# Layer 1 of a two-layer mixer trunk: the rotary exchange by GpSimd's transfers in place of ScalarE's copies

## The chip, the cores and the metric

The kernel runs on one core of one Trainium2 chip. Its time is the device time of one execution in microseconds (us), and the times below are the median of several runs and one profiled execution.

## What is computed

Two layers of a mixer over 256 latent positions and 256 context positions of width 2048, in fp32. Each layer normalizes the stream, projects it by one wide matrix, and sends the columns of the projection through three branches: a gated MLP that mixes positions, windowed attention with grouped heads (8 query heads, 2 key heads of 128), and a Fourier mix. Each branch is multiplied by its own gate, and one output projection returns to width 2048. Queries and keys of the latent positions are turned by a rotary embedding before the scores are taken:

```python
def rope_2d(x, cos, sin):
    shp = x.shape
    xf = x.astype(jnp.float32).reshape(*shp[:-1], 2, 2, ROPE_FREQS)
    rot = jnp.stack([-xf[..., 1, :], xf[..., 0, :]], axis=-2).reshape(shp)
    out = xf.reshape(shp) * cos[None, :, None, :] + rot * sin[None, :, None, :]
    return out.astype(x.dtype)
```

A head has 128 numbers in four groups of 32. For `rot`, groups 0 and 1 change places, and groups 2 and 3; the sign is in the sine table. The result leaves only the latent stream, so the context stream of the second layer (layer 1 here) gives keys and values and nothing else.

## The kernel before, in words

**How the numbers are held.** Activations lie with the width on the 128 partitions and positions along the free axis, so one query head of layer 1 is a tile of 128 partitions by 256 positions. Products are fp32 by parts: a number is split into a rounded high half (ScalarE, L615 or L566 for weights) and the low half, the remainder (VectorE, L616 or L568). A product is then three matmuls: high by high, high by low, low by high (L598, L599, L600). Wide units of layer 1 use L754 and L755.

**Layer 1's units.** `tunit1` computes 128 columns of the projection as 16 pairs of matmuls. Its weights come in two pieces of 512 KB, loaded by SyncE and split by ScalarE and VectorE three pieces ahead. The result is brought together by `joined`: ScalarE copies one part out of PSUM (L760) into a tile `join` in SBUF, of which there are two, and VectorE adds the other part (L761). Units run in the order: two key units, the values, eight query units, eight gate units.

**The turning.** `rope` (L1118 and on) has the `join` tile as `ps`. Four copies by ScalarE (L1125) put each group of 32 partitions into its partner's place in `rot`, one of four tiles that are parts of one called `mgl`. VectorE multiplies `join` by the cosines (L1127), `rot` by the sines (L1128) and adds the two (L1129). ScalarE rounds the sum to the high half, VectorE takes the low half; both are read by the scores.

**The scores.** `attention` is a generator. TensorE's order is written out by hand: after a query's unit, a clock of nominal PE time (`YQ`, 6.8 us in layer 1) decides behind which matmuls of the next units its scores are put, and the other steps of the softmax follow in the same manner. The scores of one head are two groups of three matmuls (`ps_sc`, L598 to L600): the first two read the query's high half, the third its low half. VectorE then adds the mask (L1147), takes maxima (L1149) and their least (L1159, `nm`), ScalarE takes exponentials (L1162, L1169), VectorE the reciprocal of their sums (L1172, L1173), ScalarE multiplies (L1178), and TensorE transposes the result (L1198).

**Who sets which order.** TensorE's order is the program's. In this stage the orders of VectorE, ScalarE, GpSimd and SyncE are made by a scheduler when the program is built; on the chip every engine keeps its order, and an instruction that waits holds up all that is queued behind it on its engine. Beside the heads, VectorE sums up the gate of the output in small steps (L362, L364), which are put between its other work.

**GpSimd's queue.** Before layer 1's key units GpSimd has asked for 28 transfers that add the input to a tile as they land (L1472, L1483); behind them it has one small power (L628) and then nothing until the end.

Of the kernel before, what the change touches and what calls it, by code (L numbers as in the profile page):

```python
# [16 lines left out]
S = 256  # L17
# [49 lines left out]
def trunk_kernel(ctx: ExitStack, tc: tile.TileContext, xT, xhalf, cT, wss, wsl, wmod, win, wout0, wout1, const, vec, rows,  # L67
                 wmat, bs, sink, out):
    nc = tc.nc
    V, A, G, PE, DMA = nc.vector, nc.scalar, nc.gpsimd, nc.tensor, nc.sync  # L70
# [6 lines left out]
    def sb(shape, dt, tag, bufs=1):  # L77
        cnt[0] += 1
        return pool.tile(shape, dt, tag=tag, bufs=bufs, name=f"{tag}_{cnt[0]}")

    def w2k(shape, dt=F32):
        return sb(shape, dt, "w2k", W2K)
# [71 lines left out]
    def cc(name):  # L154
        o, w = COFF[name]
        return cst[:, o - P:o - P + w]
# [457 lines left out]
    def split_into(hi, lo, src):  # L614
        A.copy(hi, src)  # L615
        V.tensor_tensor(out=lo, in0=src, in1=hi.bitcast(F32), op=ALU.subtract)  # L616
        return hi, lo
# [122 lines left out]
    def tunit(n, sl=None):  # L740

        sl = slice(0, n) if sl is None else sl
        ps = mm_ps("t")
        for k in range(KT):
            if k % 8 == 0:
                w = W.next()
            c = slice((k % 8) * P, (k % 8 + 1) * P)
            mm3(ps[:, sl], part(w, c), (hh[k][:, sl], hl[k][:, sl]), k == 0, k == KT - 1)
            later.tick(PASS * n)
        return ps  # L750
# [13 lines left out]
    def tunit1(streams):  # L764

        pss = [mm_ps("t") for _ in streams]
        for k in range(KT):
            if k % 8 == 0:
                w = W.next()
            for s, ps in zip(streams, pss):  # L770
                mm2(ps, part(w, slice((k % 8) * P, (k % 8 + 1) * P)), (hh, hl)[s][k], k)
                later.tick(PASS * S)
        return [joined(ps) for ps in pss]
# [12 lines left out]
    def layer(l):  # L786
        last = l == 1
# [4 lines left out]
        if last:  # L792
            a = sb([P, 4, 256], F32, "macc")
# [323 lines left out]
        def rope(hi, lo, ps, ctx=None):  # L1117

            if ctx is None and hi.shape[-1] > S:
                ctx = ps[:, S:T]  # L1120
            nrot[0] += 1
            rot = rots[nrot[0] % 4]
            for a in range(4):
                b = a ^ 1
                A.copy(rot[32 * a:32 * a + 32], ps[32 * b:32 * b + 32, 0:S])  # L1125
            t = w2k([P, S])
            V.tensor_tensor(out=t, in0=ps[:, 0:S], in1=cc("cos"), op=ALU.mult)  # L1127
            V.tensor_tensor(out=rot, in0=rot, in1=cc("sin"), op=ALU.mult)  # L1128
            V.tensor_tensor(out=rot, in0=rot, in1=t, op=ALU.add)  # L1129
            split_into(hi[:, LAT], lo[:, LAT], rot)  # L1130
            if hi.shape[-1] > S:
                split_into(hi[:, CTX], lo[:, CTX], ctx)
# [4 lines left out]
        def attention(h, ps):  # L1137
            g = h // 4
            q = w2k([P, n], F32R), w2k([P, n], F32R)
            rope(*q, ps)  # L1140
            yield YQ[l]
            sc, mx = [], sb([P, 4], F32, "mx", 2)
# [78 lines left out]
        for h in range(len(au), 4):  # L1221
            ps = tunit1([0])[0] if last else tunit(n)
# [3 lines left out]
        for g in range(4):  # L1226
            ps = tunit1([0])[0] if last else tunit(n)
# [3 lines left out]
        for h in range(4):  # L1231
            ps = tunit1([0])[0] if last else tunit(n)
            gate(h, ps)
        state["phase"] = f"cg{l}"
        for g in range(4):
            ps = tunit1([0])[0] if last else tunit(n)
# [6 lines left out]
        for j in range(2):  # L1243
            pss = tunit1([0, 1]) if last else [tunit(T)]
            kt.append((sb([P, T], F32R, f"kt{j}"), sb([P, T], F32R, ("ws", "bsb")[j])))
            rope(*kt[j], *pss)
# [16 lines left out]
        for h in range(8):  # L1263
            ps = tunit1([0])[0] if last else tunit(n)
# [3 lines left out]
        for h in range(8):  # L1268
            ps = tunit1([0])[0] if last else tunit(n)
# [251 lines left out]
    with tc.manual_schedule(engines={EN.PE}):  # L1521
# [47 lines left out]
        ps = sums  # L1569
# [106 lines left out]
```

## Time and profile before

| | |
|---|---|
| median of 3 runs | 1114.19 us (1113.49 to 1114.28) |
| the profiled execution | 1113.58 us, of which its span is 1111.8 us |
| TensorE's granted clock | 1.000 |
| layer 1's first and last exchange copy | 861.0 us, 962.1 us |
| scores of the first and the last query head start | 905.62 us, 966.15 us |

Times inside the profile count from the start of the span. A row of the timeline has the start, the length, the engine, the line, the operation and the tiles (written, then read), and in brackets how long the engine stood idle before it, and who released it. Since an engine starts an instruction while the last one ends, the time that an instruction really holds the engine is read from start to start. PE is TensorE, DVE VectorE, ACT ScalarE, POOL GpSimd and SP SyncE.

### The profile page before, as it was taken

How to read it: one execution, taken by the hardware profiler on the slowest of the kernel's cores; microseconds unless marked ns; L12 is line 12 of the kernel's file. 1: busy time of each engine (PE TensorE's matmuls, PEld its weight loads, DVE VectorE, ACT ScalarE, POOL GpSimd, SP SyncE). 2: the span in 40 equal slices, each digit the busy share in tenths (PEclk: the TensorE clock that was granted, in tenths of full speed). 3: DMA queues.
4: the chain of work that ended last, by engine and by line, in shares of the span. 5: the costliest groups of instructions: out<-in, count | busy, mean ns of one | idle time of the engine just before them, and what ended most of it. 6: DMA issues, size and time to landing. Idle time of an engine off the chain costs nothing. (4 is left out here: it accounts for less than half of the span.)

```text
span 1111.8 us, 17330 instructions
## 1 busy us (share of the span) xinstructions
PE 1102.6 (99%) x6437; PEld 925.4 (83%) x6437; DVE 927.2 (83%) x1609; ACT 553.3 (50%) x1060; POOL 33.3 (3%) x43
## 2 busy tenths in 40 slices
PE   8999999999999999999999999999999999999998
PEld 4787888888888888888888888988988888898886
DVE  3677799999988897989999998396989789878883
ACT  4455823322335667632533334266665379867551
POOL 1000000000000000000000000030500000000000
PEclk9999999999999999999999999999999999999999
DMA  9999765666665343466567675276956676576971
GB/s 376 414 414 409 248 194 184 190 209 212 187 208 159 124 143 115 143 195 194 160 206 220 201 225 171 95 184 202 234 168 207 217 222 198 166 241 210 313 253 75
DMA packets 75526, 235.89 MB, mean 212 GB/s; under 512 B 8481, under 2 KB 15025, under 8 KB 75441
## 3 DMA queue, kind: packets, MB, share of 16 engines
q1 hardware_dynamic: 71088, 230.31, 62.5%
q0 software_dynamic: 4064, 3.69, 2.2%
q8 instruction: 50, 0.82, 0.3%
q10 hardware_dynamic: 288, 0.79, 0.2%
q14 instruction: 36, 0.29, 0.1%
HBM read 232.65 MB, written 2.10 MB: 211 GB/s over the span
## 5 line engine op out<-in xcount | busy, mean ns | idle before, releaser
L566 ACT CAST whi<-raw 128x1024 fp32r<-128x1024 f32 (+1 forms) x210 | 216.7, 1035 | 308.9 <-PE ps_t L599 208.9
L598 PE MATMUL ps_t<-hh,whi 128*128 128x512 f32 (+1 forms) x752 | 290.6, 386 | 0.0
L600 PE MATMUL ps_t<-hh,wlo 128*128 128x512 f32 (+1 forms) x752 | 289.5, 385 | 0.0
L599 PE MATMUL ps_t<-hl,whi 128*128 128x512 f32 (+1 forms) x752 | 289.2, 385 | 0.0
L568 DVE TENSOR_TENSOR wlo<-raw,whi 128x1024 fp32r<-128x1024 f32 (+1 forms) x210 | 250.7, 1197 | 46.0 <-ACT whi L566 41.0
L323 DVE SCALAR_TENSOR_TENSOR macc<-mraw,cs,macc 128x512 f32<-128x512 f32 x360 | 251.2, 743 | 9.1 <-DMA mraw<-in_wmod_dram 8.8
L754 PE MATMUL ps_t<-hh,whi 128*128 128x512 f32 x512 | 180.7, 393 | 0.0
L600 PEld LDWEIGHTS ps_t<-hh,wlo 128*128 128x128 f32 x752 | 141.2, 188 | 28.8
L598 PEld LDWEIGHTS ps_t<-hh,whi 128*128 128x128 f32 x752 | 141.2, 188 | 26.6
L599 PEld LDWEIGHTS ps_t<-hl,whi 128*128 128x128 f32 x752 | 141.2, 188 | 26.3
L755 PE MATMUL ps_t<-hh,wlo 128*128 128x256 f32 x512 | 141.9, 277 | 0.0
L754 PEld LDWEIGHTS ps_t<-hh,whi 128*128 128x128 f32 x512 | 96.2, 188 | 19.2
L755 PEld LDWEIGHTS ps_t<-hh,wlo 128*128 128x128 f32 x512 | 96.2, 188 | 0.4
L598 PE MATMUL ps_y<-whi,hh 128*128 128x512 f32 x104 | 41.3, 397 | 0.0
L600 PE MATMUL ps_y<-whi,hh 128*128 128x512 f32 x104 | 40.6, 390 | 0.0
L599 PE MATMUL ps_y<-wlo,hh 128*128 128x512 f32 x104 | 40.5, 390 | 0.0
L615 ACT CAST w2k<-ps_tp 128x512 fp32r<-128x512 f32 x40 | 23.4, 584 | 21.0 <-PE ps_scc L599 13.6
L616 DVE TENSOR_TENSOR w2k<-ps_tp,w2k 128x512 fp32r<-128x512 f32 x40 | 27.4, 684 | 2.7 <-ACT w2k L615 1.7
L628 POOL TENSOR_TENSOR rs_b<-rs_a,mhalf 128x2 f32<-128x2 f32 (+1 forms) x7 | 6.3, 900 | 750.2 <-DVE mx L1446 582.9
L1178 ACT ACTIVATE w2k<-w2k,den 128x512 f32<-128x512 f32 (+1 forms) x48 | 28.1, 645 | 0.7 <-DVE den L1173 0.6
L833 PE MATMUL ps_av<-whi,hh 128*128 128x512 f32 x64 | 24.4, 396 | 0.2 <-ACT hh L703 0.2
L598 PE MATMUL ps_o<-w2k,vv 128*128 128x256 f32 x80 | 24.3, 304 | 0.0
(498 smaller groups left out, 1798.1 us busy)
## 6 DMA issues: line engine op xcount, KB each, us to landing
raw<-in_win_dram SPq DMA_DIRECT2D x158, 512.0 KB, 4.3
mraw<-in_wmod_dram SPq DMA_DIRECT2D x128, 512.0 KB, 4.4
raw<-in_wout_dram SPq DMA_DIRECT2D x60, 512.0 KB, 4.5
mraw<-in_wsl_dram SPq DMA_DIRECT2D x12, 512.0 KB, 7.2
yy<-in_xhalf_dram SPq DMA_DIRECT2D x7, 512.0 KB, 7.4
mg<-in_wsl_dram SPq DMA_DIRECT2D x7, 512.0 KB, 8.7
mgl<-in_wsl_dram SPq DMA_DIRECT2D x7, 512.0 KB, 9.2
yy<-in_xhalf_dram POOLq DMA_DIRECT2D x28, 128.0 KB, 7.6
```

The source lines that it names most:

```text
L323: V.scalar_tensor_tensor(out=acc[:, s], in0=w[:, kk % 2], scalar=c, in1=acc[:, s], op0=ALU.mult, op1=ALU.add)
L566: self.rounded = A.copy(ph, rc)
L568: self.last = V.tensor_tensor(out=pl, in0=rc, in1=ph.bitcast(F32), op=ALU.subtract)
L598: PE.matmul(ps, st[0], mv[0], start=start, stop=False)
L599: PE.matmul(ps, st[0], mv[1], start=False, stop=False)
L600: PE.matmul(ps, st[1], mv[0], start=False, stop=stop)
L615: A.copy(hi, src)
L616: V.tensor_tensor(out=lo, in0=src, in1=hi.bitcast(F32), op=ALU.subtract)
L754: PE.matmul(ps, w[0], h, start=k == 0, stop=False)
L755: PE.matmul(ps[:, 0:S], w[1], h[:, 0:S], start=False, stop=k == KT - 1)
L833: PE.matmul(ps, st[a], mv[b], start=start and (a, b) == (0, 0), stop=stop and (a, b) == (1, 0))
L1178: A.activation(prob[i][:, b * w:(b + 1) * w], prob[i][:, b * w:(b + 1) * w], AF.Copy, scale=den[:, c:c + 1])
```

## The change

In layer 1 the four copies of each exchange become four transfers from SBUF to SBUF, each of 32 partitions by 1 KB, asked for by GpSimd. Layer 0 keeps the copies: there the source lies in PSUM.

```diff
             for a in range(4):
                 b = a ^ 1
-                A.copy(rot[32 * a:32 * a + 32], ps[32 * b:32 * b + 32, 0:S])
+                to, of = rot[32 * a:32 * a + 32], ps[32 * b:32 * b + 32, 0:S]
+                if last:
+                    G.dma_start(to, of)
+                else:
+                    A.copy(to, of)
```

The lines behind it move down by 4: the cosine product is L1131, the sine product L1132, the sum L1133, the mask L1151, the maximum L1153, `nm` L1163. TensorE's order is the same. GpSimd's has 40 transfers more, all behind the 28 and the power. The scheduler has moved instructions on VectorE and ScalarE, and single loads on SyncE.

VectorE at the first query head, from its joined sum (`join_8940`) to its low half (`w2k_8944`), before. `mgl` is the exchanged tile, `wlo` a weight split, `ctrl` a step of the gate, `join_9004` the next head's sum:

```order
L761 TENSOR_TENSOR join_8940<-join_8940,ps_t_8891 128x256
L364 SCALAR_TENSOR_TENSOR ctrl_8792<-mraw_8962,cs_156,ctrl_8792 128x512
L1127 TENSOR_TENSOR w2k_8949<-join_8940,cst_149 128x256
L364 SCALAR_TENSOR_TENSOR ctrl_8792<-mraw_8962,cs_156,ctrl_8792 128x512
L1128 TENSOR_TENSOR mgl_8466<-mgl_8466,cst_149 128x256
L1129 TENSOR_TENSOR mgl_8466<-mgl_8466,w2k_8949 128x256
L568 TENSOR_TENSOR wlo_8985<-raw_8982,whi_1619_8984 128x1024
L616 TENSOR_TENSOR w2k_8944<-mgl_8466,w2k_8943 128x256
```

The same place on VectorE now:

```order
L761 TENSOR_TENSOR join_8940<-join_8940,ps_t_8891 128x256
L364 SCALAR_TENSOR_TENSOR ctrl_8792<-mraw_8962,cs_156,ctrl_8792 128x512
L1131 TENSOR_TENSOR w2k_8949<-join_8940,cst_149 128x256
L364 SCALAR_TENSOR_TENSOR ctrl_8792<-mraw_8962,cs_156,ctrl_8792 128x512
L568 TENSOR_TENSOR wlo_8985<-raw_8982,whi_1619_8984 128x1024
L1132 TENSOR_TENSOR mgl_8466<-mgl_8466,cst_149 128x256
L761 TENSOR_TENSOR join_9004<-join_9004,ps_t_8955 128x256
L1133 TENSOR_TENSOR mgl_8466<-mgl_8466,w2k_8949 128x256
L568 TENSOR_TENSOR wlo_9023<-raw_9020,whi_1627_9022 128x1024
L616 TENSOR_TENSOR w2k_8944<-mgl_8466,w2k_8943 128x256
```

One weight split has moved ahead of the sine product, and the next split and the next head's sum now stand between the sine product and the low half.

VectorE at the third query head (`join_9094`), from its sine product to its low half (`w2k_9098`) and the following head's sum, before. `mx` and `nm` are of the second head's scores:

```order
L1128 TENSOR_TENSOR mgl_8466<-mgl_8466,cst_149 128x256
L1149 TENSOR_REDUCE mx_9130<-ps_sc_9137 128x1
L1129 TENSOR_TENSOR mgl_8466<-mgl_8466,w2k_9103 128x256
L1159 TENSOR_SCALAR nm_9143<-mx_9130,nskb_7399 128x2
L568 TENSOR_TENSOR wlo_9165<-raw_9162,whi_1659_9164 128x1024
L616 TENSOR_TENSOR w2k_9098<-mgl_8466,w2k_9097 128x256
L761 TENSOR_TENSOR join_9194<-join_9194,ps_t_9109 128x256
```

The same place on VectorE now:

```order
L1132 TENSOR_TENSOR mgl_8466<-mgl_8466,cst_149 128x256
L1153 TENSOR_REDUCE mx_9130<-ps_sc_9137 128x1
L1133 TENSOR_TENSOR mgl_8466<-mgl_8466,w2k_9103 128x256
L1163 TENSOR_SCALAR nm_9143<-mx_9130,nskb_7399 128x2
L568 TENSOR_TENSOR wlo_9165<-raw_9162,whi_1659_9164 128x1024
L568 TENSOR_TENSOR wlo_9213<-raw_9210,whi_1671_9212 128x1024
L616 TENSOR_TENSOR w2k_9098<-mgl_8466,w2k_9097 128x256
L761 TENSOR_TENSOR join_9194<-join_9194,ps_t_9109 128x256
```

A second weight split now stands ahead of the low half; before, it stood behind the following head's sum.

## The prediction

> **What bounds the kernel now.** I read the page's busy shares first, then the table by stretches over the query stage of layer 1, then the one changed line, then the timeline head by head. On the page TensorE is busy nearly all the time:
>
> ```profile
> PE 1102.6 (99%) x6437; PEld 925.4 (83%) x6437; DVE 927.2 (83%) x1609; ACT 553.3 (50%) x1060; POOL 33.3 (3%) x43
> ```
>
> Whole-run shares mix stages, so the table by stretches decides; the eight query heads with their copies lie at about 900 to 965 us:
>
> ```profile
> 900.00:930.00 30.00, 29.99 (x173) 25.76 (x172) 28.12 (x56) 26.05 (x53) 0.00 (x0) 1.00 0.66 204
> 930.00:965.00 35.00, 34.87 (x221) 31.21 (x220) 32.63 (x71) 31.93 (x70) 0.00 (x0) 1.00 0.53 183
> ```
>
> The columns are length, busy time of PE, PEld, DVE, ACT and POOL, granted clock, DMA share, GB/s. PE is idle for 0.14 us of 65, at clock 1.00. DVE is 93% busy, ACT 89%, POOL does nothing. So PE bounds this stage. Freed ACT time can give back 0.14 us at most; the change can only cost if it makes PE wait. The copies themselves:
>
> ```profile
> L1125 ACT COPY mgl<-join x40: 400/404/408, 861.0 to 962.1; 32x256 f32<-32x256 f32 x40
>   DVE mgl L1128: 3.7, 8
> ```
>
> Forty copies of 0.40 us (16 us of ACT), four for each of two key and eight query heads. DVE's product with the sine waits for them 8 times, 3.7 us in all. Query head 0 (I count heads from 0), from its joined sum to the scores:
>
> ```profile
> 900.79 0.41 DVE L761 TENSOR_TENSOR join<-join,ps_t 128x256 f32<-128x256 f32 x1
> 901.12 0.75 DVE L364 SCALAR_TENSOR_TENSOR ctrl<-mraw,cs,ctrl 128x512 f32<-128x512 f32 x1
> 901.79 0.42 DVE L1127 TENSOR_TENSOR w2k<-join,cst 128x256 f32<-128x256 f32 x1
> 902.92 0.43 DVE L1128 TENSOR_TENSOR mgl<-mgl,cst 128x256 f32<-128x256 f32 x1
> 903.99 1.23 DVE L568 TENSOR_TENSOR wlo<-raw,whi 128x1024 fp32r<-128x1024 f32 x1 [0.19 <-PE ps_t L754]
> 905.14 0.42 DVE L616 TENSOR_TENSOR w2k<-mgl,w2k 128x256 fp32r<-128x256 f32 x1
> 905.62 0.39 PE L598 MATMUL ps_sc<-kt,w2k 128*128 128x512 f32 x1
> 906.09 0.40 PE L600 MATMUL ps_sc<-kt,w2k 128*128 128x512 f32 x1
> ```
>
> The sum is done at 901.20, the exchange at 902.92 (1.7 us), the query's low half at 905.56, and PE reads it at 906.09, in an order that is fixed and the same before and after. The slack is 0.53 us.
>
> **The change part by part.** *Removed:* 40 ACT copies, 16 us. ACT does not bound the stage, so this gives nothing by itself.
>
> *Added:* 40 requests on GpSimd, four in a row per head, and a landing. No transfer from SBUF to SBUF, nor one of 32 rows, is in this trace, so I bound the price by GpSimd's other requests and by the quickest store:
>
> ```profile
> 781.99 8.94 POOL L1483 DMA_DIRECT2D yy<-in_xhalf_dram  x10 [4.49 <-DVE yy L1482]
> L1472 POOL DMA_DIRECT2D yy<-in_xhalf_dram x1: 873/873/873, 737.7 to 737.7; - x1
> DMA to landing us min/median/max: 3.0/3.0/3.0
> ...
> L1472 POOL DMA_DIRECT2D yy<-in_xhalf_dram x1: 873/873/873, 745.1 to 745.1; - x1
> DMA to landing us min/median/max: 4.5/4.5/4.5
> ...
> L1524 POOL DMA_DIRECT2D ct<-in_cT_dram x1: 749/749/749, 1.2 to 1.2; - x1
> ...
> out_dram<-yy SPq DMA_DIRECT2D x2, 128.0 KB, 1.9
> ```
>
> Ten requests of 128 rows stand 0.89 us apart; the one that moves only 16 KB took 0.75. If all of it went by rows, 32 rows would take 0.89/4 = 0.22. I take 0.7, near the small request. Single requests of 128 KB that also add landed 3.0 to 4.5 us after their start, the quickest store 1.9 after. I take 2.7 for 32 KB: under the 3.0, since a quarter of the bytes moves and nothing is added. From the joined sum to the last landing, L = 0.05 (my allowance for the hand-over) + 3 x 0.7 + 2.7 = 4.85 us, against 1.7 us now in head 0. Bounds: 0.05 + 3 x 0.22 + 1.9 = 2.6 and 0.05 + 3 x 0.89 + 4.5 = 7.2. [...]
>
> GpSimd has nothing else queued there. What queues behind a late landing is DVE's order: behind the sine product stand the next head's sum, weight splits, maxima and the query's own low half. How long these hold DVE, start to start:
>
> ```profile
> 925.68 0.68 DVE L1149 TENSOR_REDUCE mx<-ps_sc 128x1 f32<-128x512 f32 x1
> 926.28 0.41 DVE L1129 TENSOR_TENSOR mgl<-mgl,w2k 128x256 f32<-128x256 f32 x1
> 926.61 0.22 DVE L1159 TENSOR_SCALAR nm<-mx,nskb 128x2 f32<-128x2 f32 x1
> 926.74 1.22 DVE L568 TENSOR_TENSOR wlo<-raw,whi 128x1024 fp32r<-128x1024 f32 x1
> ```
>
> A maximum 0.60, a product or sum over 256 columns 0.33, nm 0.13; a weight split 1.14 (1.15 between 903.99 and 905.14 above), an L364 step 0.67 (901.12 to 901.79). The low half lasts 0.42 to its end. Counted along DVE's new order from landing to the end of the low half, heads 0 to 7 need W = 2.55, 3.0, 4.1, 2.35, 2.9, 2.95, 2.35 and 2.95 us. (Head 0: sine product, head 1's sum, sum, split, low half = 3 x 0.33 + 1.14 + 0.42. Head 2: two splits, a maximum and nm lie in it.)
>
> When PE needs the low halves of heads 1 to 7, and where the joined sums of heads 4 and 7 start:
>
> ```profile
> 912.96 0.40 PE L600 MATMUL ps_sc<-kt,w2k 128*128 128x512 f32 x1
> 920.70 0.50 PE L600 MATMUL ps_sc<-kt,w2k 128*128 128x512 f32 x1
> 929.26 0.40 PE L600 MATMUL ps_sc<-kt,w2k 128*128 128x512 f32 x1
> 938.43 0.39 PE L600 MATMUL ps_sc<-kt,w2k 128*128 128x512 f32 x1
> 948.22 0.39 PE L600 MATMUL ps_sc<-kt,w2k 128*128 128x512 f32 x1
> 957.41 0.39 PE L600 MATMUL ps_sc<-kt,w2k 128*128 128x512 f32 x1
> 966.62 0.39 PE L600 MATMUL ps_sc<-kt,w2k 128*128 128x512 f32 x1
> 930.82 0.40 DVE L761 TENSOR_TENSOR join<-join,ps_t 128x256 f32<-128x256 f32 x1
> 959.39 0.42 DVE L761 TENSOR_TENSOR join<-join,ps_t 128x256 f32<-128x256 f32 x1
> ```
>
> A PE stall moves all later needs by its length; call the stalls so far S. The joined sum of head 1 follows head 0's landing by 0.66 in the new order; those of 2, 3, 5 and 6 stand right behind the low half before them (+0.33); those of 4 and 7 hang on PE work and keep their times of before plus S.
>
> - Head 0: sum 901.20, landed 906.05, low half 908.60, needed 906.09: stall **2.51**.
> - Head 1: 906.71, 911.56, 914.56, needed 912.96 + 2.51 = 915.47: none.
> - Head 2: 914.89, 919.74, 923.84, needed 923.21: **0.63**. S = 3.14.
> - Head 3: 924.17, 929.02, 931.37, needed 932.40: none.
> - Head 4: 931.22 + 3.14 = 934.36, 939.21, 942.11, needed 941.57: **0.54**. S = 3.68.
> - Head 5: 942.44, low half 950.24, needed 951.90; head 6: 950.57, 957.77, needed 961.09: none.
> - Head 7: 959.81 + 3.68 = 963.49, 968.34, 971.29, needed 970.30: **0.99**.
>
> Sum 4.7 us. With other L the same steps give 0.3 (2.6), 0.8 (3.15), 2.2 (4.2), 7.9 (5.5), 12.3 (6.3) and 18 (7.1): from about 5 us on every head pays. Head 0 alone stalls by L minus 2.34.
>
> *Moved and costed at nothing.* The key heads wait longer too, but their copies run from 861.0 and their results are first read at 905.62; that is over 30 us of cover. Where too little work stands ahead of the sine product, DVE stands still, and the weight splits behind it come later. Their lead covers that: the split at 926.74 is first read by the unit that starts here, 9 us later:
>
> ```profile
> 936.17 0.48 PE L754 MATMUL ps_t<-hh,whi 128*128 128x512 f32 x1
> ```
>
> If that cover went, each further us in which DVE stands still would cost PE a us. SP's order moves by single places. Below nothing: no gain over the 0.14 us of PE idle is there to be had.
>
> **The rivals.** *1. The transfers are hidden (not slower).* If L is under 4.2, for instance 0.4 per request and 2.5 to land (3.75), only head 0 stalls, by 1.4 us: 1115.6. For it: four times fewer rows than in any row of GpSimd here, and SBUF at both ends. Against: four requests one after the other, while 1.7 us serve now. The point that decides is L = 4.2, where the sum is 2.2 us, 0.2% of 1114.19, about what a measurement of this kernel can tell from no change.
>
> *2. DVE takes over as the bound.* If L is over 5.75, DVE stands still in front of each sine product for longer than the 7% that it has free, and the delay is handed from head to head through the sum that stands behind the low half. At L = 6.3: 12.3 us, 1126.5. For it: landings of 4.5 us for lone requests and a DMA share of 0.53 to 0.66. Against: those moved four times the bytes and added.
>
> [...]
>
> *4. Faster:* only if the 0.14 us stood for hidden PE time.
>
> **How the numbers follow.** Chances: the forecast (L from 4.2 to 5.75, 2 to 9 us) 0.50; hidden 0.25; DVE-bound 0.18; slow PE 0.05; faster 0.02. The profiled execution took 1113.58 us; 4.7 more is 1118.3. The median of the runs is 0.61 higher, so I predict 1114.19 + 4.7 = 1118.9. The range goes from L = 3.15 (0.8 us, 1115.0) to L = 6.2 (11.8 us, 1126.0), which leaves out about a tenth at each end. Faster by over 0.2%: 0.02; within: 0.25; slower: 0.50 + 0.18 + 0.05 = 0.73.
>
> **What would show it.** In the profile after: 40 requests on POOL about 0.7 us apart, the last of four landing 4.85 us after L761; DVE idle before its sine product with the transfer as releaser; PE idle before the scores of heads 0, 2, 4 and 7, most at head 0 (2.5 us), none inside the weight units. It would be wrong if PE waits on weights (wlo), if PE has no idle time in front of head 0's scores, if the stalls are as large in heads 1, 3, 5 and 6, or if the requests or landings are outside 2.6 to 7.2 us together.

## The result: about 1% slower

| | before | after |
|---|---|---|
| median | 1114.04 us (4 runs, 1113.49 to 1114.28) | 1125.06 us (4 runs, 1123.53 to 1126.31) |
| the profiled execution | 1113.58 us, span 1111.8 us | 1124.4 us, span 1122.6 us |
| mean granted clock of TensorE | 1.000 | 0.997 |

The ratio is 1.0100, with a 95% interval of 1.0088 to 1.0113: slower by 11.0 us. The forecast was 4.7 us. The sign and the place were right, the forecast size was less than half of the measured one. The ratios in this document leave out two executions at a far lower clock, one of the kernel before (1217 us, clock 0.85) and one of the kernel with only the key heads (6088 us, clock 0.17).

The profile after, in the order in which that of before was read. First the page's busy shares and the two stretches of the query stage:

```profile
PE 1107.2 (99%) x6437; PEld 927.0 (83%) x6437; DVE 926.6 (83%) x1609; ACT 538.0 (48%) x1020; POOL 52.9 (5%) x83
```

```profile
900.00:930.00 30.00, 26.56 (x133) 22.10 (x132) 23.74 (x49) 15.80 (x29) 7.84 (x16) 0.89 0.60 193
930.00:965.00 35.00, 32.61 (x197) 27.37 (x196) 28.56 (x61) 22.84 (x48) 5.88 (x12) 1.00 0.55 172
```

The whole-run share of PE still reads 99%; the stage tells the story. PE was idle for 0.14 us of these 65 us before; now it is idle for 3.44 us of the first 30 and 2.39 us of the next 35, and in the first its clock is 0.89 instead of 1.00. ACT's total fell by 15.3 us, about the 16 us that the copies took, and nothing came of it.

The transfers, by the view of their line:

```profile
L1127 POOL DMA_DIRECT2D mgl<-join x40: 496/496/575, 860.8 to 970.3; - x40
...
  DVE mgl L1132: 12.4, 8
...
DMA to landing us min/median/max: 1.7/3.6/5.4
```

A request costs 0.496 us where 0.7 was taken; a landing takes 1.7 to 5.4 us, 3.6 in the middle, where 2.7 was taken. DVE waits 12.4 us for them, 3.7 before. Query head 0 in the timeline (a row for POOL stands for its four requests):

```profile
900.65 0.41 DVE L761 TENSOR_TENSOR join<-join,ps_t 128x256 f32<-128x256 f32 x1
901.35 1.96 POOL L1127 DMA_DIRECT2D mgl<-join  x4 [27.77 <-DVE join L761]
907.50 0.43 DVE L1132 TENSOR_TENSOR mgl<-mgl,cst 128x256 f32<-128x256 f32 x1 [3.64 <-DMA mgl<-join]
909.08 0.79 PE L598 MATMUL ps_sc<-kt,w2k 128*128 128x512 f32 x1 [3.44 <-ACT w2k L615]
910.12 0.79 PE L600 MATMUL ps_sc<-kt,w2k 128*128 128x512 f32 x1
```

From the end of the joined sum (901.06) to the sine product 6.44 us pass, against a forecast L of 4.85. PE waits 3.44 us for the high half and reads the low half 910.12 - 906.09 = 4.03 us later than before. And the matmul, 0.39 us long before, now takes 0.79. The clock in that neighbourhood, in a table by stretches:

```profile
907.00:908.00 1.00, 0.00 (x0) 0.00 (x0) 0.50 (x2) 0.00 (x0) 0.00 (x0) 1.00 0.60 246
908.00:909.00 1.00, 0.00 (x0) 0.00 (x0) 1.00 (x3) 0.38 (x1) 0.46 (x1) 0.51 0.01 4
909.00:914.00 5.00, 4.92 (x13) 3.71 (x14) 3.85 (x9) 0.10 (x2) 1.50 (x4) 0.50 0.45 133
914.00:915.00 1.00, 1.00 (x5) 0.85 (x5) 0.79 (x3) 0.98 (x2) 0.00 (x0) 0.57 0.00 0
915.00:920.00 5.00, 5.00 (x30) 4.34 (x29) 3.78 (x8) 4.57 (x10) 1.58 (x4) 1.00 0.52 174
```

The clock halves at about 908.0, while PE still stands idle, and is back at about 914.85. PE works from 909.08 to 914.85 at half speed. The low halves of heads 1 to 7, to be held against the rows of before:

```profile
919.27 0.40 PE L600 MATMUL ps_sc<-kt,w2k 128*128 128x512 f32 x1
926.78 0.50 PE L600 MATMUL ps_sc<-kt,w2k 128*128 128x512 f32 x1
936.17 0.51 PE L600 MATMUL ps_sc<-kt,w2k 128*128 128x512 f32 x1 [0.25 <-DVE w2k L616]
948.05 0.50 PE L600 MATMUL ps_sc<-kt,w2k 128*128 128x512 f32 x1 [0.30 <-DVE w2k L616]
958.17 0.50 PE L600 MATMUL ps_sc<-kt,w2k 128*128 128x512 f32 x1 [0.42 <-DVE w2k L616]
967.47 0.39 PE L600 MATMUL ps_sc<-kt,w2k 128*128 128x512 f32 x1
977.28 0.50 PE L600 MATMUL ps_sc<-kt,w2k 128*128 128x512 f32 x1 [0.44 <-DVE w2k L616]
```

Each row's start less that of before is how far PE has fallen behind; the step from head to head is what that head cost. L is taken here as the start of the sine product less the end of the joined sum; where DVE came to the product only after the landing, it is an upper bound.

| head | 0 | 1 | 2 | 3 | 4 | 5 | 6 | 7 |
|---|---|---|---|---|---|---|---|---|
| behind, us | 4.03 | 6.31 | 6.08 | 6.91 | 9.62 | 9.95 | 10.06 | 10.66 |
| step, us | 4.03 | 2.28 | -0.23 | 0.83 | 2.71 | 0.33 | 0.11 | 0.60 |
| L, us | 6.44 | 5.65 | at most 4.51 | 6.69 | 5.46 | 6.83 | at most 4.30 | 5.75 |
| landing, median us | 4.1 | 1.7 | 2.6 | 5.0 | 4.1 | 4.6 | 2.4 | 1.7 |
| DMA share around it | 0.94 | 0.30 | 0.62 | 0.88 | 0.87 | 0.82 | 0.42 | 0.56 |

The span ends 10.8 us later, so all of the loss arises at these eight heads. Head 1's step is not a wait: PE stands nowhere between the low halves of heads 0 and 1, and the 2.28 us are the slow clock. The last two rows are the four transfers of a head and the DMA share of 4 or 5 us around their requests, cut at whole microseconds: above 0.8 the middle landing takes 4.1 to 5.0 us, below 0.65 it takes 1.7 to 2.6, though the last of the four, for which DVE waits, took 3.8 and 3.9 us at heads 1 and 7. Two of these heads in the views, the landings first:

```profile
DMA to landing us min/median/max: 1.7/1.7/3.8
...
DMA to landing us min/median/max: 4.5/5.0/5.4
```

```profile
908.00:912.00 4.00, 2.92 (x7) 2.00 (x8) 3.27 (x7) 0.41 (x1) 1.96 (x4) 0.50 0.30 58
927.00:932.00 5.00, 5.00 (x32) 4.47 (x32) 4.13 (x11) 2.97 (x6) 1.96 (x4) 1.00 0.88 313
```

These are heads 1 and 3: the same transfers, with 58 and 313 GB/s in all on the DMA engines. The share is a rough sign and no law: in the kernel with fewer loads (below) head 5's middle landing was 4.2 us at a share of 0.57 (943 to 948 us), and before the change the request of 128 KB that landed in 3.0 us did so at 0.98 (737 to 741 us).

### The profile page after: what moved, and what is told of

Read it like the earlier page. It is cut to its first block, busy times and chain, and to the rows that moved or that the text cites. A ratio compares the mean times of both kernels' runs of the same rounds, so it can differ in the third digit from the quotient of the medians.

```text
span 1122.6 us, 17381 instructions
## 1 busy us (share of the span) xinstructions
PE 1107.2 (99%) x6437; PEld 927.0 (83%) x6437; DVE 926.6 (83%) x1609; ACT 538.0 (48%) x1020; POOL 52.9 (5%) x83
## 5 line engine op out<-in xcount | busy, mean ns | idle before, releaser
L1127 POOL DMA_DIRECT2D mgl<-join x40 | 19.7, 499 | 133.5 <-DVE join L761 79.7
```

## Experiments

My theory after the result: the loss is the lateness of the sine product behind landings that are slow because weight loads share the DMA engines; a stall of head 0 adds a stretch of half clock; everything else about the change is free. The rivals: the relief of ScalarE and the moved orders cost something themselves; GpSimd's path is the slow one; or the place of the wait in VectorE's order matters more than its length. The ratios are to the kernel before on the same chip, run beside them. One limit holds for all of these kernels but one: the scheduler makes its orders of VectorE and ScalarE anew for each. Through the query stage they are those of the changed kernel only in the kernel with fewer loads; elsewhere part of a difference may be the new order's.

**Only the key heads by transfers.**

```diff
-                if last:
+                if last and nrot[0] < 3:
                     G.dma_start(to, of)
```

> Only the two key heads use the transfers. Theory (their results are read 30 us later, the cover is complete): 1114.0 us, no change. Rival (VectorE standing still in front of the key heads' sine product delays weights or queries behind it): 1115 to 1117 us.

Measured: 1113.61 us against 1113.61, ratio 1.0001 (0.9991 to 1.0011). Their cover holds, as costed.

**No exchange at all.**

```diff
-                if last:
-                    G.dma_start(to, of)
-                else:
+                if not last:
                     A.copy(to, of)
...
-            V.tensor_tensor(out=rot, in0=rot, in1=cc("sin"), op=ALU.mult)
+            V.tensor_tensor(out=rot, in0=ps[:, 0:S] if last else rot, in1=cc("sin"), op=ALU.mult)
```

> Layer 1 leaves out the exchange altogether: the sine product reads the joined tile itself, so ScalarE is relieved of its 40 copies as in the change, and no transfer is waited for (the turned queries and keys are then not those of the reference). Theory (all of the loss comes from the wait for the landings and what it sets off; the relief of ScalarE and the moved orders cost and give nothing): 1113.4 to 1114.2 us, PE without a wait over 0.3 us between 895 and 985 us. Rival (the orders of VectorE and ScalarE that the scheduler makes without the copies are themselves worse): 1118 us or more, with PE waits at the scores.

Measured: 1112.94 us against 1113.71, ratio 0.9993 (0.9983 to 1.0003). The query stage in the table by stretches:

```profile
895.00:985.00 90.00, 90.00 (x556) 80.31 (x554) 81.02 (x164) 65.50 (x128) 0.00 (x0) 1.00 0.65 205
```

PE is busy for 90.00 of 90 us. The time is 0.8 us below that of before and a little below the expected range; the interval reaches from 1.9 us less to 0.3 us more, so what the relief of ScalarE is worth cannot be told from nothing. The order that the scheduler made here does no harm where nothing is waited for. It is not the changed kernel's order, so this points to the wait and does not prove it.

**Fewer loads beside the transfers.** In layer 1 the gate's sums read 4 loads of 512 KB instead of 32; the other 28 are left out and the sums read old data.

```diff
-                if kk % 2 == 0:
+                if kk == 0:
                     w = sb([P, 2, 512], F32, "mraw", 2)
```

> Leaves out 28 of the 32 loads of 512 KB that the summing of the output's gate makes beside the query heads (the sums then read old data). Theory (a transfer of the exchange lands late because weight loads are in flight on the same DMA engines): the landings, median 3.6 us, fall to about 2.5 us, and the time from 1125.1 to about 1118 us. Rival (the landing time is GpSimd's own path): landings stay at 3.6 us and the time at 1125 us.

Measured: 1118.59 us against 1113.92, ratio 1.0042 (1.0025 to 1.0059). The transfers in the list of DMA issues (the last number is the median from issue to landing, us) and PE's waits, both for the query stage:

```profile
mgl<-join POOLq DMA_DIRECT2D x32, 32.0 KB, 3.3
```

```profile
PE ps_sc L598 <- ACT w2k L615: 2.9, 2, 2.5
PE ps_sc L600 <- DVE w2k L616: 1.0, 3, 0.4
```

In the changed kernel the median in this stretch was 3.8 and the first wait 4.5 us in two, 3.4 the longest. The time is the expected one, though the landing fell to 3.3 us and not to 2.5. TensorE, VectorE and ScalarE keep the changed kernel's orders through the query stage, so the two differ there in the loads alone: loads beside the transfers lengthen them, and with 0.5 us less of landing more than half of the loss is gone. After a wait of 2.5 us the clock stayed at 1.00 here.

**The same transfers asked for by ScalarE.**

```diff
-                    G.dma_start(to, of)
+                    A.dma_start(to, of)
```

> The same 40 transfers, asked for by ScalarE instead of GpSimd. Theory (weight loads in flight set the landing): landings of 2 to 5 us as before, TensorE still waits in front of head 0's scores for some 3 us, about 1122 to 1125 us. Rival (GpSimd's way of asking, 0.49 us each and a slow landing, is the cost): landings near 2 us, about 1116 us.

Measured: 1124.50 us against 1113.92, ratio 1.0095 (1.0080 to 1.0110), the same as the change within the intervals.

```profile
mgl<-join ACTq DMA_DIRECT2D x32, 32.0 KB, 3.9
```

The landing is that of GpSimd's transfers, 3.9 against 3.8. Who asks does not matter here.

**Two requests in a row in place of four.**

```diff
-                    G.dma_start(to, of)
+                    (G if a % 2 else A).dma_start(to, of)
```

> The changed kernel, with two of the four transfers of each exchange asked for by GpSimd and two by ScalarE, so that two requests stand in a row in place of four, about 1 us less. Theory (the requests in series and the landing add up, and only their sum counts): from the joined sum to the sine product of head 0 about 5.4 us in place of 6.4, each other head that waits about 1 us less; the steps of the prediction with these values give about 4 us of stalls, so 1117.5 to 1120.5 us. Rival (the landings are set by the loads that share the DMA engines, and four transfers in flight at once land as late as before): still 6 us or more at head 0 and 1123 us or more.

Measured: 1125.70 us against 1113.67, ratio 1.0102 (1.0085 to 1.0118). The sine product of head 0 came 5.90 us after its sum, 0.54 us sooner, not 1 us. The landings over the run, and PE's waits:

```profile
DMA to landing us min/median/max: 1.7/3.8/6.2
```

```profile
PE ps_sc L598 <- ACT w2k L615: 6.7, 3, 2.8
PE ps_sc L600 <- DVE w2k L616: 1.8, 3, 1.0
```

The time is the rival's, though its 6 us at head 0 were 5.90. The longest landing grew from 5.4 to 6.2 us, the scheduler put the sum of head 2 later on VectorE, where PE now waited 2.76 us, and the clock halved twice for 3.4 us (from 911.2 and from 959.0). The term of 0.5 us per request could not be cashed; which of these undid it, this run does not separate.

**GpSimd copies, with no transfer.**

```diff
-                    G.dma_start(to, of)
+                    G.tensor_copy(out=to, in_=of)
```

> No transfers at all: GpSimd itself copies the four groups, ScalarE stays relieved as in the change. Theory (the whole loss is the transfers' wait; ScalarE's relief and the orders that follow from it are worth nothing either way): 1113.6 us if a copy takes under some 0.6 us, up to 2 us more otherwise. Rival (the rearranged orders on VectorE and ScalarE cost by themselves): 1118 us or more.

Measured: 1120.11 us against 1113.92, ratio 1.0055 (1.0040 to 1.0070): my theory missed, and the time is the one of the rival that I had put on record, that the moved orders cost by themselves. Head 2 in the timeline:

```profile
914.92 2.69 POOL L1127 COPY mgl<-join 32x256 f32<-32x256 f32 x4 [4.85 <-DVE join L761]
917.64 0.42 DVE L1132 TENSOR_TENSOR mgl<-mgl,cst 128x256 f32<-128x256 f32 x1 [1.65 <-POOL mgl L1127]
919.97 1.33 ACT L1182 ACTIVATE w2k<-w2k,den 128x512 f32<-128x512 f32 x2 [2.67 <-DVE den L1177]
920.75 0.33 PE L1202 MATMUL ps_tp<-identr,w2k 128*128 128x128 f32 x1 [1.74 <-ACT w2k L1182]
```

Four copies take GpSimd 2.69 us where four by ScalarE took 1.6. VectorE stands 1.65 us in front of head 2's sine product, and behind it in its order waits head 0's reciprocal (L1177), which ScalarE's scaling and then PE's transposes need. PE waits 1.74 us for another head's work, and its clock is at half from 922.4 to 925.8. I read this as the third rival, partly right: what a wait costs depends on what is queued behind the waiting instruction. That moved orders cost without any wait is not what the kernel with no exchange showed; but its order is another one than here, so the two are not fully separated.

**Only head 0 by transfers, and all but head 0.** The condition is `last and nrot[0] == 3`, and `last and nrot[0] != 3`; the rest stays with ScalarE's copies.

> Query head 0 alone uses the transfers; everything else keeps ScalarE's copies. Theory: 1114.0 + 6.4, about 1120.4 us, with TensorE's clock at half behind a wait of about 3.4 us. Rival (all heads pay alike): about 1115.4 us.

> Query head 0 alone gets its copies by ScalarE back; the key heads and query heads 1 to 7 keep the transfers. Theory (head 0's stall of 3.5 us and the slow clock behind it, 2.9 us, are over half of the loss, since head 0 has the least cover): 1125.1 - 6.4, about 1118.7 us. Rival (all eight query heads pay alike, 11/8 = 1.4 us each): about 1123.7 us.

Measured: only head 0 gives 1121.20 us, ratio 1.0067 (1.0052 to 1.0082), near the expected 1120.4; all but head 0 gives 1122.30 us, ratio 1.0077 (1.0062 to 1.0092), far above my theory's 1118.7 (before: 1113.61). Its interval, 1120.5 to 1123.9 us, still holds the 1123.7 of the rival that all heads pay alike, but the first kernel, 5.8 us above that rival's 1115.4, does not fit it. PE's waits in the query stage, with head 0 alone:

```profile
PE ps_sc L598 <- ACT w2k L615: 5.2, 2, 4.2
PE ps_sc L600 <- DVE w2k L616: 0.6, 1, 0.6
```

And without head 0:

```profile
PE ps_sc L598 <- ACT w2k L615: 2.7, 3, 1.3
PE ps_sc L598 <- ACT w2k L1173: 2.1, 2, 1.9
PE ps_sc L600 <- DVE w2k L616: 2.1, 5, 0.6
```

The two losses are 7.6 and 8.7 us, 16.3 together, and the whole change costs 11.0. Without head 0's stall, head 1 waits 1.31 us and head 3 2.31 us (1.90 of it for ScalarE's exponentials), where the changed kernel waits 0 and 0.25. A stall at head 0 gives every later exchange that much more time; taken away, the later heads wait in its place. The prediction's own steps say so: with the L's that the changed kernel showed they give 9.4 us, and with no stall at head 0, head 1's sum ending at 906.82 as it does here, still 7.9, since head 1 then stalls by 2.5. The landings moved as well: L is 7.6 and 7.0 us here at heads 3 and 4, in the changed kernel 6.7 and 5.5.

**Work for PE during the wait.** Twelve matmuls whose results are overwritten stand ahead of head 0's scores; in a second kernel eight more stand ahead of head 2's.

```diff
                 s = mm_ps("sc")
+                for _ in range({0: 12, 2: 8}.get(h, 0) if last and b == 0 else 0):
+                    PE.matmul(s, kt[g][0][:, 0:P], kt[g][0], start=True, stop=True)
```

> Twelve matmuls whose result is overwritten (some 0.23 us each, 2.8 us in all) stand on TensorE ahead of query head 0's scores, where it idles 3.4 us in the changed kernel. Theory (head 0's late query idles TensorE long enough for its clock to halve): the clock stays at 1.00 and the 2.9 us that head 0's scores and the next unit lose at half clock come back: about 1122.2 us. Rival (the clock costs nothing, all of it is waiting): about 1125 us, as the changed kernel.

> Twelve overwritten matmuls ahead of head 0's scores and eight ahead of head 2's, the two places where TensorE idled over 2 us with the first twelve alone. Theory (half clock costs about 2 us wherever it strikes): the clock stays at 1.00 from 900 to 940 us, about 1124 us against 1126.2 with the first twelve alone. Rival (what is won at one head is waited for at the next): about 1126 us although the clock stays up.

Measured: 1126.24 us, ratio 1.0113 (1.0098 to 1.0128), for the first, which missed; 1124.47 us, ratio 1.0094 (1.0079 to 1.0109), for the second, near the expected 1124, though the interval's upper end still holds the rival's 1126. The first kernel's clock, at head 0 and then at head 2:

```profile
905.00:920.00 15.00, 13.70 (x70) 11.06 (x70) 10.12 (x23) 5.97 (x13) 1.96 (x4) 1.00 0.57 189
925.00:929.00 4.00, 1.61 (x6) 1.04 (x7) 3.50 (x8) 2.23 (x6) 1.96 (x4) 1.00 0.62 174
929.00:932.00 3.00, 3.00 (x11) 2.50 (x10) 2.05 (x7) 0.80 (x1) 0.00 (x0) 0.51 0.86 329
```

(The first kernel has only the twelve.) Head 0's slow stretch is gone: the scores of head 1 start 7.5 us after those of head 0, in the changed kernel 9.7 us. But head 2's scores then waited 2.27 us, and the clock fell there instead; in the new order of VectorE head 2's sum ended at 919.83, 1.7 us later than in the changed kernel. With both places filled the clock reads 1.00 throughout the stage, and the time is 0.6 us below the change's, within the intervals. So the slow clock is real, but what it costs in the end is not shown. A gain of 0.6 us would fit a slow stretch that is mostly cover for later heads; the two intervals are too wide to exclude the whole 2.28 us, and the new orders come on top.

**Head 0's scores 2.5 us later, and all heads' 0.5 us later,** in nominal time of TensorE's order.

```diff
-            yield YQ[l]
+            yield YQ[l] + (2.5 if last and h == 0 else 0)
...
-            yield YA[l]
+            yield YA[l] - (2.5 if last and h == 0 else 0)
```

For all heads, `YQ` of layer 1 is 7.3 in place of 6.8.

> The changed kernel, with only the scores of query head 0 put 2.5 us of nominal PE time later in TensorE's order; the steps behind them keep their places. Head 0's low half is then late by about 1 us in place of 3.4, and the slow clock does not come at head 0. Theory (a stall of PE at one head is cover for the heads behind it, so that what is saved at head 0 is waited for later, as where head 0 kept its copies, 1122.3): 1121 to 1123.5 us, with PE waiting at heads 1 to 5 for more than the 3.9 us that the changed kernel waits there. Rival (stalls simply add): 3.4 - 1.0 + 2.9 = 5.3 us less than the changed kernel, 1119.7 us or less.

> The changed kernel, with the scores of all eight query heads 0.5 us of nominal PE time later in TensorE's order. Theory (each stall is the lateness of a low half against a fixed place, and a later place helps at every head that waits; the slow clock at head 0 still comes, since 2.9 us of waiting remain): 0.5 us less at head 0 and little more than that in sum, since the needs behind it move too, 1123 to 1125 us. Rival (0.5 us off at each of the heads 0, 3, 4, 5 and 7, where the changed kernel waits): 2.5 us less, 1122.5 us or less.

Measured: 1126.56 us, ratio 1.0119 (1.0101 to 1.0137), and 1143.96 us, ratio 1.0261 (1.0240 to 1.0282), against 1113.71: both above either theory. PE's waits of the first, then of the second:

```profile
PE ps_sc L598 <- ACT w2k L615: 4.3, 4, 1.6
PE ps_sc L600 <- DVE w2k L616: 1.7, 3, 0.7
PE ps_o L599 <- DVE w2k L616: 1.6, 2, 1.4
```

```profile
PE ps_o L598 <- ACT w2k L615: 8.3, 5, 3.1
PE ps_o L599 <- DVE w2k L616: 6.2, 5, 1.4
PE ps_sc L598 <- ACT w2k L615: 3.3, 1, 3.3
```

With head 0 later, its wait fell from 3.44 to 1.18 us, heads 1 and 4 took over (1.58 and 1.01, and 0.62 and 0.75 more for their low halves), and the clock fell at both. With all heads later, the scores of seven heads no longer wait at all; the outputs of the softmax (`ps_o`), whose steps stand behind the scores on VectorE and ScalarE, wait 14.5 us. The clock halved at four places, for 23.9 us together. A later place for the scores moved the wait one step down the chain. How much of the 30 us is the scheduler's new order, how much the clock and how much the landings is not separated, and so it is with the 12.9 us of the first.

## Why the prediction was right in sign and too small

**What bounds the stage: right.** PE, with no gain from a relieved ScalarE that can be told from nothing; shown by the kernel with no exchange.

**The landing: the step that failed.** "I take 2.7 for 32 KB: under the 3.0, since a quarter of the bytes moves and nothing is added." Fewer bytes did not land sooner: 3.8 us in the middle over the query stage, and 4.1 to 5.0 at the four heads where the DMA share is over 0.8. The row of 4.5 us was the nearer one. Nothing in the two rows told which to take, since both requests stood beside loads (DMA share 0.98 around the one of 3.0, 0.73 around the one of 4.5), so going below the lower of them had no ground. By the prediction's own table an L of 5.5 costs 7.9 us and one of 6.3 costs 12.3; the measured 11.0 lies between. The requests went the other way, 0.50 instead of 0.7, 1.5 instead of 2.1 us for three, and made up 0.6 us of it.

**One L for all heads: wrong.** L was 5.5 to 6.8 us at the six heads where DVE waited and under 4.6 at heads 2 and 6.

**The way from L to stalls: right in the sum, less so by head.** I put the measured L's, at their bounds for heads 2 and 6, into the prediction's own steps, with its own W. Head 0 is 901.20 + 6.44 + 2.55 - 906.09 = 4.10. All stalls come out as 4.10, 0, 1.09, 0.81, 1.15, 0.32, 0 and 1.89 us, 9.4 in all, where the span grew by 10.8. For the kernel with fewer loads, whose L's are 5.51, 5.38, at most 3.56, 5.22, 4.73, 5.96, at most 4.25 and 5.91 us, they give 3.17, 0.42 (head 4) and 2.05 (head 7), 5.6 in all, and its span grew by 1117.3 - 1111.8 = 5.5. Head 0's 4.10 was 4.03 in the trace. The places are less exact: I had PE waiting at heads 0, 2, 4 and 7, and it waited at 0, 3, 4, 5 and 7. Head 4's step was 2.71 against 1.15, since VectorE, busy without a gap, reached its sum 8.4 us later than before where PE was only 6.9 behind; head 7's was 0.60 against 1.89. With fewer loads it is the same, 1.35 against 0.42 and 0.76 against 2.05. The errors at these two heads nearly cancel, and head 2's 1.09 did not come at all (its step is -0.23, behind the 2.28 us of slow clock at head 1); that the sums come so close is in part luck. The steps also belong to the changed kernel's order: for the kernel with two requests in a row, which has another, they give at most 7.8 us where the span grew by 13.4.

**Rival 2, the delay handed on, was half right.** The sums of heads 3, 5 and 6 do stand right behind late low halves. But heads do not fail alone: each stall is cover for the next, which the steps hold through S, and which I forgot when I expected the experiments with and without head 0 to add up.

**The slow PE, given 0.05, came true.** No run shows how long a stall has to be for it. In the changed kernel the clock halved at 908.03 us, inside head 0's wait of 3.44 us. It costs 2.28 us where it stands. The sum with the measured L's leaves 10.8 - 9.4 = 1.4 us over, which fits a slow stretch partly taken as cover by later heads; that split is argued, not shown: with the clock held at 1.00 the time was 0.6 us lower, within the intervals.

**Costed at nothing and right:** key heads, SP's order, no wait of PE inside the weight units.

## What to carry to other kernels

A small transfer inside SBUF is not sure to land sooner than a large one when it shares the DMA engines with a stream of loads (here 32 KB took 1.7 to 5.4 us, and two requests of 128 KB 3.0 and 4.5): price its landing by the spread of the transfers that land beside the same loads, and carry that spread through to the forecast. Here copies of 0.40 us on ScalarE, 89% busy over the query stage, left PE idle for 0.14 us of 65, and relieving ScalarE of them brought nothing that could be measured (0.8 us without the exchange, within the interval); what counted was the length of the chain from producer to consumer. When one late step serves as cover for the next, experiments that remove one of them do not add up, so put the measured lateness through the whole order before naming a cause.

## What the hardware showed beside it

The half clock came in stretches of about 3.4 us or twice that. In the changed kernel it lasted from 908.03 to 914.85, in the kernel with head 0 filled from 929.04 to 932.45, and at two places of the kernel with head 0's scores later 3.41 us each, from 918.29 and from 949.01 (mean clock in stretches there):

```profile
918.00:922.00 4.00, 4.00 (x16) 3.37 (x15) 3.57 (x9) 2.48 (x6) 1.95 (x4) 0.57 0.69 251
949.00:952.00 3.00, 3.00 (x10) 2.42 (x9) 3.00 (x9) 1.92 (x4) 1.65 (x4) 0.50 0.77 209
```

No wait by its length alone decides it: a wait of 2.27 us at head 2 was followed by half clock, one of 2.52 us (fewer loads) was not; with two requests in a row one of 2.70 us was (to 909.11), one of 2.76 us was not (to 929.24); and in the kernel with head 0's scores later waits of 1.58 and 0.62 us, 1.4 us apart, were enough. At 929.04, 918.29 and 949.01 us, the three places above, PE was already back at work when the clock fell.

Nor does PE's busy time in the 4 us before the clock fell (in the last two rows, 4 us behind which it did not), cut at whole microseconds:

| kernel | 4 us of the span | PE busy in them, us | clock after them |
|---|---|---|---|
| head 0 filled | 925 to 929 | 1.61 | half from 929.04 |
| changed | 904 to 908 | 1.64 | half from 908.03 |
| head 0's scores later | 914 to 918 | 1.79 | half from 918.29 |
| GpSimd copies | 918 to 922 | 1.98 | half from 922.4 |
| head 0's scores later | 945 to 949 | 2.25 | half from 949.01 |
| fewer loads | 905 to 909 | 1.32 | full |
| all but head 0 | 931 to 935 | 1.70 | full |

Neither figure tells the falls from the rest, and why the clock fell at some of these places and not at others is left open.
